# RWKV-7 and HGRN2 layer on one core: the turns of beta,k, of v and of RWKV's outputs made of 32x32 blocks by way of DRAM, and a thread for each pair's end

## The chip, the cores and the metric

One core of a Trainium2 chip. The metric is the device time in microseconds of one launch; the median of three runs counts. Everything is float32; the large products split each operand into a high part (fp32r) and the rest.

## The reference

One layer over T = 512 frames of width 2048 (batch 1):

```
proj = x @ w_in                                      # 512 x 8320
RWKV-7 (16 heads of 64, in the kernel 8 pairs of heads of 128 channels):
  r,k,v,z (+ low-rank decay w and gate a), token shift on all
  S_t = S_{t-1} diag(w_t) + (S_{t-1} a_t) b_t^T + v_t k_t^T ;  o_t = S_t r_t
  o  = groupnorm(o) * gn_w + gn_b + sum(r*k*r_k) * v
  out_r = o * silu(z)
HGRN2 (8 heads of 128): gated linear recurrence, chunkwise; out_h = rmsnorm(o) * g_norm_w * silu(z)
y = [out_r ; out_h] @ w_out
x <- LayerNorm(ALPHA * x + y)
```

## The kernel before

**Stages.** Channels lie on partitions and time on the free axis (128 x 512 tiles). The projections come in units of 128 columns (`proj`, 16 steps of three matmuls each), in the order of `_order()`: for each group of two pairs k, r, v, the z of the group before, then q, f and g of two HGRN heads. Every weight tile (`wr`, 128 x 1024) is loaded on SP's queue and split on chip, half by half, into `wh` (ACT) and `wl` (DVE); there are three buffers of each. A split is asked for one to two parts ahead of its use (`ready`), and the second split of a tile issues the load of the tile after next. After the projections come four output products of 512 columns (`rows`): each has 16 steps, one for each 128 rows of the gated outputs, with 12 matmuls (4 blocks of time, 3 products each).

**RWKV.** `rwkv_prep` makes a pair's operands: `ar` (alpha, r), `bk` (beta, k), both 128 x (8 chunks, 128), the scores `sc`, and turns beta,k and v from channels by time to time by channels, chunk by chunk: `bk` in place, v into rows 64 to 127 of `zz`. `turned` does this without PE: DVE transposes 32 x 32 blocks within each group of partitions (`dtr`), then DMAs between SBUF tiles carry the blocks to their partitions: 16 DMAs of 32 KB for beta,k, 8 for v, in four lots. `rwkv_invert` inverts the triangular part, `from_v` makes the first products of `zz`; `rwkv_scan` goes through the eight chunks of two pairs at once; `outputs` adds what the scores and `zz` give. `rwkv_finish` is a pair's end: mean and variance per head in layout time by channels (`o_all`, in the buffer `ot`), then four identity transposes on PE into a PSUM bank (`tr`, L328), which two scalar_tensor_tensors read together with the weight, `bv`, the bias and the gate; `put_gated` hands the result `g` over. Twelve of the sixteen gated tiles are stored to DRAM (`spill`) and reloaded; RWKV's pairs 6 and 7 and HGRN's heads 6 and 7 stay in `g` buffers, of which there are four.

**Order of work.** All instructions are issued by one planner (class `Plan`) while the program is built. It keeps a clock for each engine, with a cost for each operation, and for each tile the time at which it is ready. The stream of large matmuls is the main line; after each matmul `pump` lets the waiting threads (generators in queues: splits, evacuations, scans, groups, ends, preparations, heads, stores) issue what is due. A PE operation is issued when its operands are due 0.35 us before now, an operation of another engine when they are due within 0.5 us from now. The engines then execute in that order. A thread may wait for room in a pool (`room`), for a tile (`landed`, `by_now`) or for a time. `plan.ready[name] = (time, "dma")` is what the planner takes as landing; on the chip, semaphores hold the readers back until the data is there. All `dma_start` calls of the stretches that matter go through SP's queue, in the order of issue; the planner's `turned` does not look at what else is on that queue.

**The first output product.** At step j, `ahead(j, 0)` splits the gated tile of step j+1 (`split_gated(j + 2)`), whose order is 0 to 5, 8 to 13, 14, 6, 15, 7 (`korder`; 6 and 7 are RWKV's last pairs, 8 and up are HGRN's heads). At step 8 it loads the LayerNorm weights, `lnw` (tile `big`, from `ln_wb`, broadcast to all partitions); from step 11 on it also loads the residual rows (`g<-x_r`). The weight part of step j+2 is split when step j is half issued.

```python
        if d == 0:
            split_gated(j + 2)
            if j == 8:
                plan.until(room(big=1))
                lnw.append(take("big", [P, 2, D]))
                nc.sync.dma_start(lnw[0], ln_wb[None].to_broadcast([P, 2, D]))
```

Of the kernel before, what the change touches and what calls it, by code (L numbers as in the profile page):

```python
# [241 lines left out]
def mixer_kernel(ctx, tc, head, x_r, w_all, par, up, ln_wb, consts, hmask, out):  # L242
# [41 lines left out]
    def drop(*tiles):  # L284
        for t in tiles:
            name = t.tensor.name
            plan.slots[tags.pop(name)].append((plan.used.get(name, plan.count), plan.busy[name][0]))
# [77 lines left out]
    def dtr(o, i):  # L365
        return dve_op([i], o, lambda: dve.transpose(o, i), per=0.0019)
# [22 lines left out]
            f = lambda: dve.tensor_copy(o, i)  # L389
        return Op([act_way(o, i, AF.Copy, scale), ("dve", 0.075 + size(o) * 0.00105 + moved(o, i), f)], [i], [o])  # L390

    def turned(dst, src, tmp, rows=4, base=0):


        name = dst.tensor.name
        yield dtr(tmp, src)
        yield lambda: by_now(tmp)
        for a in range(4):
            for b in range(rows):
                o = base + 32 * b  # L400
                nc.sync.dma_start(dst[o : o + 32, :, 32 * a : 32 * a + 32],
                                  tmp[32 * a : 32 * a + 32, :, 32 * b : 32 * b + 32])
            at = plan.clock["pe"] + 0.4 * rows
            yield lambda: plan.clock["pe"] >= at
        plan.ready[name] = (plan.clock["pe"] + 3.0, "dma")

# [211 lines left out]
            ups.append(upw)  # L620

    hc = [slice(64 * h, 64 * h + 64) for h in range(2)]

    def rwkv_prep(S, p):
        if p == 0:
# [94 lines left out]

        yield room(q4=1)
        tmp = take("q4", [P, NCH, P])
        yield from turned(bk, bk, tmp)
        drop(tmp)
        yield has(S, "v")
        yield room(ksq=2)
        rh, rl = (take("ksq", [P, T], F32R) for _ in range(2))
# [9 lines left out]
        S["bv"] = r  # L737

        yield room(zz=1)
        z = take("zz", [P, NCH, P])  # L740
        yield room(ksq=1)
        tmp = take("ksq")
        yield from turned(z, chunks(v), chunks(tmp), rows=2, base=64)
        drop(v, tmp)
        S["zz"] = z

    def from_v(SS, sc):

        yield lambda: all("zz" in S for S in SS)
        zs = [S["zz"] for S in SS]  # L750
        yield room(main=2, mix=1)
        yield landed(*zs, sc)
        pss = [take("main") for _ in SS]
        for half, (z, ps) in enumerate(zip(zs, pss)):
            for c in range(NCH):
                for h in range(2):
                    yield mm(ps[hc[h], c * C : c * C + C], sc[64:128, 0, half * 16 + 2 * c + h],
                             z[64:128, c, hc[h]])

        def keep():  # L760
            for z, ps in zip(zs, pss):
                for h in range(2):
                    yield copy(z[0:64, :, hc[h]], chunks(ps[hc[h]]))
                drop(ps)

        return keep

    def outputs(SS, sc):

        yield room(mix=2)  # L770
        pss = [take("mix") for _ in SS]
        for half, (S, po) in enumerate(zip(SS, pss)):
            z = S["zz"]
            yield lambda z=z: by_now(z)
            for c in range(0, NCH, 2):
                for h in range(2):
                    for e in range(2):
                        yield mm(po[hc[e], c // 2 * P + 64 * h : c // 2 * P + 64 * h + 64],
                                 sc[:, 1, half * 16 + 2 * (c + e) + h], z[:, c + e, hc[h]])
        for S, po in zip(SS, pss):  # L780
            yield tt(S["o"], S["o"], tiles(po), ALU.add)
            drop(po, S["zz"])
# [49 lines left out]
    def rwkv_scan(SS, sc):  # L832

        pcs, ars, bks, zzs, os = ([S[n] for S in SS] for n in ("pc", "ar", "bk", "zz", "o"))
        yield room(bd=4, rt=2)
        bdss = [[take("bd", [P, P]) for _ in range(2)] for _ in SS]
        rts = [take("rt", [P, P]) for _ in SS]  # L840

        def block(ps, h):
            return ps[hc[h], h * 64 : h * 64 + 64]

        for rt, bds, o in zip(rts, bdss, os):
            yield memset(rt[64:128], 0.0)
            for t in bds:
                yield memset(t, 0.0)
            yield memset(o[0:64, 0], 0.0)
        olds = [None] * 2  # L850
        for c in range(NCH):
            more = c < NCH - 1
            zs = [zz[:, c] for zz in zzs]
            news = [bds[c % 2] for bds in bdss]
            pxs = []
            if c > 0:
                yield landed(*olds)
                yield room(mix=2)
                for ar, old in zip(ars, olds):
                    pxs.append(take("mix"))  # L860
                    yield mm(pxs[-1][:, :P], ar[:, c], old)
                for rt, px, z in zip(rts, pxs, zs):
                    yield stt(rt[0:64], px[0:64, :P], -1.0, z[0:64], ALU.mult, ALU.subtract)
                if more:
                    for new, old, pc in zip(news, olds, pcs):
                        yield act(new, old, AF.Copy, scale=pc[:, c : c + 1])
            else:
                for rt, z in zip(rts, zs):
                    yield copy(rt[0:64], z[0:64], scale=-1.0)
            yield landed(*rts)  # L870
            yield room(mix=2)
            psas = [take("mix") for _ in SS]
            for half, (psa, rt) in enumerate(zip(psas, rts)):
                i = half * 16 + 2 * c
                yield mm(psa[:, :P], sc[:, 0, i : i + 2].rearrange("p h t -> p (h t)"), rt)
            for psa, z in zip(psas, zs):
                for h in range(2):
                    yield copy(z[0:64, hc[h]], block(psa, h))
                drop(psa)
            for px, o in zip(pxs, os):  # L880
                yield copy(o[64 * (c % 2) : 64 * (c % 2) + 64, c // 2], px[64:128, :P])
                drop(px)
            if more:
                yield landed(*zzs)
                yield room(mix=2)
                pds = [take("mix") for _ in SS]
                for pd, bk, z in zip(pds, bks, zs):
                    yield mm(pd[:, :P], bk[:, c], z)
                for pd, new, pc in zip(pds, news, pcs):
                    for h in range(2):  # L890
                        yield stt(new[hc[h], hc[h]], block(pd, h), pc[hc[h], c : c + 1],
                                  new[hc[h], hc[h]], ALU.mult, ALU.add)
                    drop(pd)
                olds = news
        drop(*ars, *bks, *pcs, *rts, *bdss[0], *bdss[1])

    def rwkv_finish(S, p):

        o_all = S["o"]
        yield room(sm=1, ksq=1)  # L900
        og = o_all.rearrange("p j (h i) -> p (j h) i", i=64)
        sm = take("sm", [P, 3, 8])
        sq = take("ksq", [P, 8, 64])
        yield red(sm[:, 0], og)
        yield ts(sm[:, 0], sm[:, 0], 1.0 / 64, None, ALU.mult)
        yield tt(og, og, sm[:, 0, :, None].to_broadcast([P, 8, 64]), ALU.subtract)
        yield act(sq, og, AF.Square)
        yield red(sm[:, 1], sq)
        yield ts(sm[:, 1], sm[:, 1], 1.0 / 64, GN_EPS, ALU.mult, ALU.add)
        yield rsqrt(sm[:, 2], sm[:, 1])  # L910
        yield tt(og, og, sm[:, 2, :, None].to_broadcast([P, 8, 64]))
        drop(sm, sq)
        yield has(S, "z", "bv")
        yield room(g=1, ksq=1)
        g = take("g")
        sz = take("ksq")
        z = S["z"]
        yield landed(o_all)
        po = take("mix")
        for j in range(4):  # L920
            yield tr(po[:, j * P : j * P + P], o_all[:, j])
        yield act(sz, z, AF.Tanh, scale=0.5)
        yield stt(g, po, hcol(HGW, p), S["bv"], ALU.mult, ALU.add)
        drop(po)
        yield stt(z, sz, 1.0, z, ALU.add, ALU.mult)
        yield stt(g, g, hcol(HGB, p), z, ALU.add, ALU.mult)
        drop(z, S["bv"], S["ot"], sz)
        put_gated(p, g)

    def rwkv_group(SS, grp):  # L930
        yield lambda: all("scored" in S for S in SS)
        sc = scores[grp]
        yield from rwkv_invert(SS, sc)

        def run():
            yield from rwkv_scan(SS, sc)
            yield from outputs(SS, sc)
            drop(sc)
            for i, S in enumerate(SS):
                plan.add(finishes, rwkv_finish(S, 2 * grp + i))  # L940

        plan.add(scans[0], run())

# [186 lines left out]


    scans = [plan.queue(), plan.queue()]
    groups, finishes, preps = plan.queue(), plan.queue(), plan.queue()
    heads, stores = plan.queue(), plan.queue()


# [530 lines left out]
```

## Time and profile before

| | |
|---|---|
| median of 3 runs | 1050.75 us (1050.46 to 1051.28) |
| profiled execution | 1050.24 us, of it 1048.5 us from first to last instruction |
| granted TensorE clock | 0.999 |
| PE busy | 1040.6 us (99%), 7342 matmuls |
| DVE, ACT, POOL busy | 755.7 (72%), 437.6 (42%), 38.3 (4%) us |
| DMA moved | 114.79 MB, 56368 of 87305 packets under 512 B |

The profile names a group of instructions by line, engine, operation and tiles (out<-in, buffer numbers left out; a PE matmul names the moving operand, then the stationary one), with count, busy time and the mean duration of one. A line is often that of a helper (L453 the large products in `three`, L324 `mm`, L328 `tr`, L337/L338 ACT passes, L347 tensor_tensor, L356 scalar_tensor_tensor, L366 the block transpose, L401 the DMAs in `turned`, L430 the weight loads), so the tile's name tells the place. The timeline's rows have start, duration, engine, line, what it is, how many were merged, and in brackets how long the engine had been idle and who released it. PE's durations are modelled and overlap; distances between starts are what counts.

### The profile page before, as it was taken

What the parts mean: (1) busy time and instruction counts of PE and PEld (TensorE: products, weight loads), DVE (VectorE), ACT (ScalarE), POOL (GpSimd) and SP (SyncE); (2) the same over time, 40 slices, a digit from 0 to 9 for tenths busy, and PEclk for the clock granted to TensorE, in tenths of its full rate; (3) what the DMA queues carried; (4) which work ended last, traced back from release to release, by engine and by line L of the source; (5) the groups of instructions that cost most, each with busy time, mean ns of one, the idle gap of its engine ahead of it and who ended that gap; (6) DMA issues with size and microseconds to landing.
All of it is one profiled execution on the core that took longest, in us unless ns stands there. A gap on an engine that the chain in (4) does not pass through costs nothing.

```text
span 1048.5 us, 18840 instructions
## 1 busy us (share of the span) xinstructions
PE 1040.6 (99%) x7342; PEld 865.1 (83%) x7342; DVE 755.7 (72%) x1653; ACT 437.6 (42%) x867; POOL 38.3 (4%) x81
## 2 busy tenths in 40 slices
PE   9999999999999999999999999999999999999997
PEld 8888888888888888888888888888888888888885
DVE  7465898667759987676689866865998778625556
ACT  6545333445353354452533353525334554323321
POOL 0000000000000000000000000000000002000000
PEclk9999999999999999999999999999999999999999
DMA  8134342222343522223534323234352244545613
GB/s 332 54 103 114 99 109 86 86 79 81 84 123 100 122 82 74 78 98 79 138 78 118 98 62 96 70 96 110 100 128 72 69 164 131 182 131 159 202 60 131
DMA packets 87305, 114.79 MB, mean 109 GB/s; under 512 B 56368, under 2 KB 58160, under 8 KB 87088
## 3 DMA queue, kind: packets, MB, share of 16 engines
q1 hardware_dynamic: 87072, 113.39, 36.6%
q8 instruction: 58, 0.95, 0.4%
q14 instruction: 31, 0.25, 0.1%
q10 hardware_dynamic: 144, 0.20, 0.1%
HBM read 99.92 MB, written 7.34 MB: 102 GB/s over the span
## 4 chain that ended last, share of the span: by engine, by line
PE 99%; DVE 1%; DVEq 0%; issue 0%
PE main L453 74%; PE mix L324 11%; PE mix L453 8%; PE main L1192 3%; PE main L324 2%; PE mix L328 1%; PE mix L1142 0%; DVE inv L356 0%; DVE inv L347 0%; DVE stats L1549 0%; DVEq L1663 0%; DVE mv L1357 0%; DVE bd L356 0%; DVE mv L352 0%; DVE inv L1140 0%
## 5 line engine op out<-in xcount | busy, mean ns | idle before, releaser
L453 PE MATMUL main<-xl,wh 128*128 128x512 f32 x864 | 341.1, 395 | 0.0
L453 PE MATMUL main<-xh,wl 128*128 128x512 f32 x864 | 341.1, 395 | 0.0
L453 PE MATMUL main<-xh,wh 128*128 128x512 f32 x864 | 340.9, 395 | 0.0
L337 ACT ACTIVATE wh<-wr 128x512 fp32r<-128x512 f32 x299 | 186.9, 627 | 237.1 <-PE main L453 180.5
L347 DVE TENSOR_TENSOR wl<-wr,wh 128x512 fp32r<-128x512 f32 x299 | 203.8, 682 | 61.8 <-ACT wh L337 60.1
L453 PEld LDWEIGHTS main<-xh,wh 128*128 128x128 f32 x864 | 162.4, 188 | 33.0
L453 PEld LDWEIGHTS main<-xh,wl 128*128 128x128 f32 x864 | 162.5, 188 | 32.6
L453 PEld LDWEIGHTS main<-xl,wh 128*128 128x128 f32 x864 | 162.4, 188 | 32.6
L453 PE MATMUL main<-wl,xh 128*128 128x512 f32 (+1 forms) x262 | 102.6, 392 | 0.0
L453 PE MATMUL main<-wh,xh 128*128 128x512 f32 (+1 forms) x262 | 102.1, 390 | 0.0
L453 PE MATMUL main<-wh,xl 128*128 128x512 f32 (+1 forms) x262 | 101.6, 388 | 0.0
L453 PEld LDWEIGHTS main<-wh,xh 128*128 128x128 f32 x262 | 49.2, 188 | 9.9
L453 PEld LDWEIGHTS main<-wh,xl 128*128 128x128 f32 x262 | 49.2, 188 | 9.7
L453 PEld LDWEIGHTS main<-wl,xh 128*128 128x128 f32 x262 | 49.2, 188 | 9.6
L338 ACT ACTIVATE t<-main,om 128x512 f32<-128x512 f32 x33 | 22.4, 687 | 51.1 <-PE main L453 41.6
L356 DVE SCALAR_TENSOR_TENSOR t<-main,pr,t 128x511 f32<-128x511 f32 x33 | 24.4, 747 | 26.5 <-ACT t L338 26.2
L347 DVE TENSOR_TENSOR inv<-inv,inv 64x30 f32<-64x30 f32 (+14 forms) x120 | 38.6, 322 | 2.9
L347 DVE TENSOR_TENSOR inv<-inv 64x30 f32<-64x30 f32 (+14 forms) x120 | 38.4, 320 | 2.3
L347 DVE TENSOR_TENSOR t<-t,tot 128x256 f32<-128x256 f32 x96 | 37.8, 414 | 1.8 <-PE mix L324 1.7
L356 DVE SCALAR_TENSOR_TENSOR bd<-mix,pc,bd 64x64 f32<-64x64 f32 x112 | 31.7, 283 | 7.5 <-PE mix L324 5.2
L337 ACT ACTIVATE zz<-mix 64x64 f32<-64x64 f32 x63 | 13.8, 220 | 46.9 <-PE mix L324 45.8
L338 ACT ACTIVATE t<-main 128x512 f32<-128x512 f32 x32 | 18.5, 598 | 30.7 <-PE main L453 30.2
(222 smaller groups left out, 1328.0 us busy)
## 6 DMA issues: line engine op xcount, KB each, us to landing
wr<-w_all SPq DMA_DIRECT2D x156, 512.0 KB, 3.6
q<-head SPq DMA_DIRECT2D x15, 448.0 KB, 5.9
q<-q SPq DMA_DIRECT2D x128, 32.0 KB, 2.4
g<-x_r SPq DMA_DIRECT2D x16, 256.0 KB, 3.8
spill<-g SPq DMA_DIRECT2D x12, 256.0 KB, 2.7
out<-q SPq DMA_DIRECT2D x12, 256.0 KB, 2.4
t<-spill SPq DMA_DIRECT2D x10, 256.0 KB, 4.2
zz<-ksq SPq DMA_DIRECT2D x64, 32.0 KB, 2.6
```

Source lines behind the costliest of these rows:

```text
L324: return Op([("pe", cost, lambda: pe.matmul(o, l, r, start=start, stop=stop, **kw))], [l, r], [o], mode="narrow" if narrow else "main" if ...
L328: return Op([("pe", 0.11, lambda: pe.transpose(o, i, ident))], [i], [o])
L337: return "act", cost, lambda: sc_e.activation(o, i, f, scale=scale)
L338: return "act", cost, lambda: sc_e.activation(o, i, f, scale=scale, bias=bias)
L347: return dve_op([a, b], o, lambda: dve.tensor_tensor(o, a, b, f), base=0.16 if o.shape[0] < P and size(o) == C and o.tensor.name in tags e ...
L356: return dve_op([a, b], o, lambda: dve.scalar_tensor_tensor(o, a, s, b, f1, f2), per=0.00113, base=0.085 if o.shape[0] == P else 0.25 if s ...
L453: pe.matmul(ps, l, r, start=first and i == 0, stop=last and i == 2)
L1192: pe.matmul(pss[a], *ops, start=k == 0 and low == of == 0, stop=k == KT - 1 and low == 1)
```

## The change

`turned` now makes a turn of a tile of c chunks by n groups of 32 columns in three steps: one `dtr` whose output lies block column by block column; one DMA of the whole tile to a new DRAM tile `far`; then, 4.4 us of planned PE time later, n DMAs back (4 for beta,k and for an end, 2 for v), each bringing one block row to 32 partitions, with contiguous pieces of c x 32 numbers. The planner takes the target as ready 4.7 us after these are issued. The turned layout has block columns outside and chunks inside: (a, c, f) in place of (c, a, f). `zz` is kept in that layout and its readers use strided views; beta,k is copied by ACT or DVE into the other layout, into the buffer that held the block transpose. In `rwkv_finish` the four PE transposes go: `o_all` is block-transposed into `g`, goes by way of DRAM back into `ot`, one ACT pass applies weight and bias while reordering, and two tensor_tensors add `bv` and multiply by the gate. The queue of ends becomes two queues, one for each pair of a group.

```diff
+    def turned(dst, src, tmp, base=0):
+        c = src.shape[1]
+        n = src.shape[2] // 32
+        yield dtr(tmp, src.rearrange("p c (b f) -> p b c f", f=32))
         yield lambda: by_now(tmp)
-        for a in range(4):
-            for b in range(rows):
-                o = base + 32 * b
-                nc.sync.dma_start(dst[o : o + 32, :, 32 * a : 32 * a + 32],
-                                  tmp[32 * a : 32 * a + 32, :, 32 * b : 32 * b + 32])
-            at = plan.clock["pe"] + 0.4 * rows
-            yield lambda: plan.clock["pe"] >= at
-        plan.ready[name] = (plan.clock["pe"] + 3.0, "dma")
+        far = dpool.tile([4, 32, n, c * 32], F32, tag=nm("far"), name=nm("far"))
+        nc.sync.dma_start(far.rearrange("a p b r -> (a p) b r"), tmp.rearrange("p b c f -> p b (c f)"))
+        plan.busy[tmp.tensor.name] = (plan.clock["pe"] + 4.4, "dma")
+        at = plan.clock["pe"] + 4.4
+        yield lambda: plan.clock["pe"] >= at
+        for b in range(n):
+            o = base + 32 * b
+            nc.sync.dma_start(dst[o : o + 32].rearrange("p a c f -> p a (c f)"),
+                              far[:, :, b].rearrange("a p r -> p a r"))
+        plan.ready[dst.tensor.name] = plan.busy[dst.tensor.name] = (plan.clock["pe"] + 4.7, "dma")
...
-        yield from turned(bk, bk, tmp)
-        drop(tmp)
+        flat = bk.rearrange("p c t -> p (c t)")
+        yield from turned(blocks(flat, NCH), bk, blocks(tmp.rearrange("p c t -> p (c t)"), NCH))
+        yield copy(tmp.rearrange("p c (a f) -> p a c f", f=32), blocks(flat, NCH))
+        drop(bk)
+        S["bk"] = tmp
...
-        z = take("zz", [P, NCH, P])
+        z = take("zz", [P, 4, NCH, 32])
...
-        yield from turned(z, chunks(v), chunks(tmp), rows=2, base=64)
+        yield from turned(z, chunks(v), blocks(tmp, NCH), base=64)
...
-                             z[64:128, c, hc[h]])
+                             z[64:128, hb[h], c])
...
-        yield room(g=1, ksq=1)
+        yield room(g=1)
         g = take("g")
+        yield from turned(blocks(S["ot"], 4), o_all, blocks(g, 4))
+        yield room(ksq=1)
         sz = take("ksq")
         z = S["z"]
-        yield landed(o_all)
-        po = take("mix")
-        for j in range(4):
-            yield tr(po[:, j * P : j * P + P], o_all[:, j])
         yield act(sz, z, AF.Tanh, scale=0.5)
-        yield stt(g, po, hcol(HGW, p), S["bv"], ALU.mult, ALU.add)
-        drop(po)
+        yield act(in_blocks(g), blocks(S["ot"], 4).rearrange("p a c f -> p c a f"), AF.Identity,
+                  scale=hcol(HGW, p), bias=hcol(HGB, p))
         yield stt(z, sz, 1.0, z, ALU.add, ALU.mult)
-        yield stt(g, g, hcol(HGB, p), z, ALU.add, ALU.mult)
+        yield tt(g, g, S["bv"], ALU.add)
+        yield tt(g, g, z)
...
-                plan.add(finishes, rwkv_finish(S, 2 * grp + i))
+                plan.add(finishes[i], rwkv_finish(S, 2 * grp + i))
...
-    groups, finishes, preps = plan.queue(), plan.queue(), plan.queue()
+    groups, finishes, preps = plan.queue(), [plan.queue(), plan.queue()], plan.queue()
```

The other readers and writers of `zz` (`from_v`, `outputs`, `rwkv_scan`) change their views in the same way.

More of the change, by code (lines that the diff above doesn't have):

```diff
@@ L390, in copy, with in_blocks, blocks @@
         return Op([act_way(o, i, AF.Copy, scale), ("dve", 0.075 + size(o) * 0.00105 + moved(o, i), f)], [i], [o])
-    def turned(dst, src, tmp, rows=4, base=0):
-        name = dst.tensor.name
-        yield dtr(tmp, src)
+    def turned(dst, src, tmp, base=0):
+        c = src.shape[1]
+        n = src.shape[2] // 32
+        yield dtr(tmp, src.rearrange("p c (b f) -> p b c f", f=32))
         yield lambda: by_now(tmp)
-        for a in range(4):
-            for b in range(rows):
-                o = base + 32 * b
-                nc.sync.dma_start(dst[o : o + 32, :, 32 * a : 32 * a + 32],
-                                  tmp[32 * a : 32 * a + 32, :, 32 * b : 32 * b + 32])
-            at = plan.clock["pe"] + 0.4 * rows
-            yield lambda: plan.clock["pe"] >= at
-        plan.ready[name] = (plan.clock["pe"] + 3.0, "dma")
+        far = dpool.tile([4, 32, n, c * 32], F32, tag=nm("far"), name=nm("far"))
[8 more added lines that the diff above has]
+        plan.ready[dst.tensor.name] = plan.busy[dst.tensor.name] = (plan.clock["pe"] + 4.7, "dma")
+    def in_blocks(t):
+        return t.rearrange("p (c a f) -> p c a f", a=4, f=32)
+    def blocks(t, c):
+        return t.rearrange("p (a c f) -> p a c f", c=c, f=32)
     splits = plan.queue()
@@ L622, in mixer_kernel @@
     hc = [slice(64 * h, 64 * h + 64) for h in range(2)]
+    hb = [slice(2 * h, 2 * h + 2) for h in range(2)]
     def rwkv_prep(S, p):
@@ L762, in keep @@
                 for h in range(2):
-                    yield copy(z[0:64, :, hc[h]], chunks(ps[hc[h]]))
+                    yield copy(z[0:64, hb[h]], ps[hc[h]].rearrange("p (c a f) -> p a c f", c=NCH, f=32))
                 drop(ps)
@@ L778, in outputs @@
                         yield mm(po[hc[e], c // 2 * P + 64 * h : c // 2 * P + 64 * h + 64],
-                                 sc[:, 1, half * 16 + 2 * (c + e) + h], z[:, c + e, hc[h]])
+                                 sc[:, 1, half * 16 + 2 * (c + e) + h], z[:, hb[h], c + e])
         for S, po in zip(SS, pss):
@@ L843, in block, with by32 @@
             return ps[hc[h], h * 64 : h * 64 + 64]
+        def by32(t):
+            return t.rearrange("p (a f) -> p a f", f=32)
         for rt, bds, o in zip(rts, bdss, os):
@@ L852, in rwkv_scan @@
             more = c < NCH - 1
-            zs = [zz[:, c] for zz in zzs]
+            zs = [zz[:, :, c] for zz in zzs]
             news = [bds[c % 2] for bds in bdss]
@@ L862, in rwkv_scan @@
                 for rt, px, z in zip(rts, pxs, zs):
-                    yield stt(rt[0:64], px[0:64, :P], -1.0, z[0:64], ALU.mult, ALU.subtract)
+                    yield stt(by32(rt[0:64]), by32(px[0:64, :P]), -1.0, z[0:64], ALU.mult, ALU.subtract)
                 if more:
@@ L868, in rwkv_scan @@
                 for rt, z in zip(rts, zs):
-                    yield copy(rt[0:64], z[0:64], scale=-1.0)
+                    yield copy(by32(rt[0:64]), z[0:64], scale=-1.0)
             yield landed(*rts)
@@ L877, in rwkv_scan @@
                 for h in range(2):
-                    yield copy(z[0:64, hc[h]], block(psa, h))
+                    yield copy(z[0:64, hb[h]], by32(block(psa, h)))
                 drop(psa)
```

## The prediction

> **What bounds the kernel now.** I read the page first: busy times, then the chain that ended last, then who waited for whom on PE. From the page:
>
> ```profile
> PE 1040.6 (99%) x7342; PEld 865.1 (83%) x7342; DVE 755.7 (72%) x1653; ACT 437.6 (42%) x867; POOL 38.3 (4%) x81
> PE 99%; DVE 1%; DVEq 0%; issue 0%
> ```
>
> All waits of PE, and two pieces of the chain:
>
> ```profile
> PE mix L324 <- ACT ksq L1409: 1.5, 1, 1.5
> PE mix L1142 <- DVE inv L1140: 1.1, 1, 1.1
> PE mix L324 <- DVE bd L356: 0.4, 1, 0.4
> ...
> 893.81 13.43 PE main L453 x59
> 907.23 43.52 PE mix L453 x192
> ```
>
> PE is never out of work: its three waits come to 3.0 us, 1.1 at the start and 1.5 in the closing normalisation. So there are two ways to change the time: give PE less to do, or make it wait. DVE (72%) and ACT (42%) set the time only where PE stands and waits for them. One large matmul costs PE 43.52/192 = 0.2267 us; I use this, not the modelled durations, which overlap.
>
> **What the change takes from PE.** The four identity transposes of each pair's end go (`tr` in rwkv_finish). On PE's timeline such a batch reads:
>
> ```profile
> 280.48 0.39 PE L453 MATMUL main<-xh,wl 128*128 128x512 f32 x1
> 280.71 0.60 PE L328 MATMUL mix<-cst,t 128*128 128x128 f32 x4
> 281.06 0.48 PE L453 MATMUL main<-xh,wh 128*128 128x512 f32 x1
> 281.38 0.40 PE L453 MATMUL main<-xl,wh 128*128 128x512 f32 x1
> ...
> 893.21 0.60 PE L328 MATMUL mix<-cst,t 128*128 128x128 f32 x4
> ```
>
> Three starts later, 0.90 us have gone where two large matmuls need 0.45, so a batch costs 0.45 us, its change of kind included. I looked at all eight (first and last shown): each stands alone between large matmuls, so none keeps its change of kind when it goes. Sum: 8 x 0.45 = **-3.6 us**.
>
> **What it changes in PE's other work.** The matmuls that read `zz` now read runs of 32 columns 1 KB apart. No row shows that pattern; the nearest are short strided runs and plain ones:
>
> ```profile
> L324 PE MATMUL mix<-zz,q 128*128 128x128 f32 x112 | 17.2, 276 | 0.0
> L324 PE MATMUL mix<-zz,big 128*64 128x64 f32 x256 | 8.3, 224 | 0.0
> L324 PE MATMUL main<-zz,big 64*64 64x64 f32 x256 | 8.3, 220 | 0.0
> L324 PE MATMUL mix<-t 128*32 128x16 f32 x512 | 5.9, 185 | 0.0
> L324 PE MATMUL mix<-q,t 128*32 128x48 f32 x256 | 3.6, 208 | 0.0
> ```
>
> Plain reads lie on a line: (276-208)/80 = 0.85 ns a column, hence 181 ns for 16. The strided 16 take 185, 4 ns more. Over 112+256+256 = 624 matmuls that is +2.5 us at most; nothing at least, since a longer run can't be worse than a short one. I take 0: 4 ns is noise, and the runs here are longer.
>
> **DVE, ACT and the queues.** The block transposes of beta,k and v stay; one of 128x512 per end is new:
>
> ```profile
> L366 DVE STREAM_TRANSPOSE q<-q x8: 1231/1234/1239, 72.7 to 755.9; 128x1024 f32<-128x1024 f32 x8
> L366 DVE STREAM_TRANSPOSE ksq<-t x8: 698/700/706, 83.4 to 771.4; 128x512 f32<-128x512 f32 x8
> ```
>
> DVE gets 8 x 0.70 for it; two scalar_tensor_tensors per end become two tensor_tensors of the same size (0). ACT gets one 128x512 pass per end, 8 x 0.63 (row at 890.50 below). The new 128x1024 copy of beta,k is about two such passes on either engine, 8 x 1.3. Some 16 us in all on two engines with 255 and 611 us free: no time, as long as nobody waits in line behind them. POOL gets nothing. SP issues 5 + 3 + 5 = 13 DMAs per pair for 16 + 8 = 24, larger ones. What transfers take over the run, issue to landing:
>
> ```profile
> wr<-w_all SPq DMA_DIRECT2D x156, 512.0 KB, 3.6
> q<-q SPq DMA_DIRECT2D x128, 32.0 KB, 2.4
> spill<-g SPq DMA_DIRECT2D x12, 256.0 KB, 2.7
> t<-spill SPq DMA_DIRECT2D x10, 256.0 KB, 4.2
> zz<-ksq SPq DMA_DIRECT2D x64, 32.0 KB, 2.6
> big<-ln_wb SPq DMA_DIRECT2D x1, 2048.0 KB, 10.1
> ```
>
> A store lands in 2.7 to 3.6 and the code leaves 4.4 us for it; the returns (256 KB, or 512 KB in four pieces) come in about 4, where it leaves 4.7. So landings hold in ordinary stretches, and beta,k and v are done up to 4 us later than now. For v the margin is these rows of `zz`:
>
> ```profile
> L401 SPq DMA_DIRECT2D zz<-ksq x64: 585/608/1270, 86.8 to 778.3; - x64
> L337 ACT ACTIVATE zz<-main x8: 591/592/594, 182.1 to 800.6; 64x512 f32<-64x512 f32 x8
> ```
>
> The last block is issued at 778.3, and the first product read from it is evacuated at 800.6: some 18 us to spare. I put 0 there. What is new in kind: before, only PE read a turned tile. Now ACT or DVE copies beta,k and ACT scales the end straight from the landing, and both run in order: if it is late, all behind them is.
>
> **The one stretch where a landing is late.** It is the ends of pairs 6 and 7, beside the first output projection. That has 16 steps of 12 matmuls (2.72 us); its last ends at 907.23, so step 12 starts at 896.35 and step 13 at 899.07. Step 13 needs pair 6's gated output, step 15 pair 7's. DVE's timeline (sum of pair 6, its normalisation's last step, its gated output, that of pair 7), then SP's and ACT's:
>
> ```profile
> 872.67 0.68 DVE L360 TENSOR_REDUCE sm<-t 128x8 f32<-128x512 f32 x1
> ...
> 878.83 0.69 DVE L347 TENSOR_TENSOR t<-t,sm 128x512 f32<-128x512 f32 x1
> ...
> 883.33 0.75 DVE L356 SCALAR_TENSOR_TENSOR g<-g,half,t 128x512 f32<-128x512 f32 x1
> ...
> 895.28 0.75 DVE L356 SCALAR_TENSOR_TENSOR g<-g,half,t 128x512 f32<-128x512 f32 x1
> ```
>
> ```profile
> 884.70 0.33 SPq L430 DMA_DIRECT2D wr<-w_all  x1
> 885.13 1.26 SPq L1473 DMA_DIRECT2D big<-ln_wb  x1
> 890.09 0.33 SPq L430 DMA_DIRECT2D wr<-w_all  x1
> ```
>
> ```profile
> 890.50 0.63 ACT L337 ACTIVATE wh<-wr 128x512 fp32r<-128x512 f32 x1 [1.60 <-PE main L453]
> 891.04 0.62 ACT L337 ACTIVATE xh<-g 128x512 fp32r<-128x512 f32 x1
> 893.18 0.63 ACT L337 ACTIVATE wh<-wr 128x512 fp32r<-128x512 f32 x1 [1.00 <-PE main L453]
> 893.72 0.61 ACT L337 ACTIVATE xh<-g 128x512 fp32r<-128x512 f32 x1
> 896.54 0.63 ACT L337 ACTIVATE wh<-wr 128x512 fp32r<-128x512 f32 x1 [2.21 <-DMA wr<-w_all]
> ```
>
> Of the weight loads that SP issues between 880 and 900:
>
> ```profile
> DMA to landing us min/median/max: 3.7/4.2/6.3
> ```
>
> The 2 MB of `ln_wb` go out at 885.13 and land at 895.2. The load issued at 890.09 is the 6.3: it lands at 896.4 behind them, and ACT waits 2.2 us for it. What is issued after `ln_wb` arrives after it.
>
> Now pair 6 after the change. Its normalisation ends at 879.5 as before, or up to a microsecond later, as pair 7 now shares DVE. Transpose to 880.2; the store goes out at about 880.8 and lands by 883.6. The returns follow 4.4 us after it, 885.2 at the earliest, and `ln_wb` belongs to the start of step 8, issued some 0.4 us earlier than now, since pair 6's batch on PE is gone: 884.7. So the returns queue behind 2 MB and land not at 889.9, as the order of work assumes, but between 895.2 and about 897; I take 896.4, like the weight load.
>
> PE reaches steps 12 and 13 by then 0.9 us sooner relative to this (two batches gone): 895.45 and 898.2. Lower end: pair 6 alone is late. Scale, two DVE passes, split, 0.6 each: 896.4 + 2.4 = 898.8, a wait of **0.6**. Upper end: the scale stands in ACT's order ahead of the weight split of 890.50 and the split of 891.04, both wanted by step 12. It does, if the planner lets it go half a microsecond ahead of 889.9, as it may; that weight split belongs to the middle of step 10, 891.4 by then. ACT then stands still until 896.4, and works off scale, weight split, gated split by 898.2; DVE does pair 6's two passes and two subtractions by 899.5, of which step 12's third matmul, 0.45 in, needs the last: step 12 starts at 899.1, a wait of **3.7**. (Pair 7's returns, about 3 us later, block ACT again, but PE is late by then itself.) The row of 890.50 against 889.9 puts me near the upper end: **+3.5**.
>
> **Sum:** -3.6 + 3.5 = -0.1. The profiled execution took 1050.24 (span 1048.5 and 1.7 around it), 0.5 under the median 1050.75 of the three runs; it becomes about 1050.1, and against the median 1050.7. A difference under 0.2% (2.1 us) is about what this kernel's measurement can't tell from none.
>
> **Rivals.** First, *full gain*: the returns are there in time, because they slip ahead of `ln_wb` (half a microsecond decides) or because it clears the rings sooner. With the 4.2 us of an ordinary 256 KB load they would land at 889.4, nobody waits, and the time is 1050.75 - 3.6 = 1047.1. Against it stands the 10.1 us row and the load of 6.3 behind it. The Trainium skill, *DMA: Bandwidth & Descriptors*, section "Anatomy of one DMA", gives a transfer as about 2.0 us plus bytes over 436 GB/s (a fit for GpSimd's path); my estimate from it is 6.8 us for `ln_wb`, which would end at 891.9, the returns near 893, and the stall would all but vanish. This trace's 10.1 us disagrees, and decides. Chance of this rival 0.28, partial gains beyond 2.1 us included.
>
> Second, *SP held*: pair 7's store falls behind `ln_wb` too, lands at about 896.4, and its returns stand in SP's order ahead of the weight load of 890.09. SP then waits at the returns, and that load goes out at 896.4 + 4 x 0.33 = 897.7 for 890.09, landing 3.7 later at 901.4 against 896.4. Split by 902.7, it feeds step 14, due at 895.45 + 5.44 = 900.9, or 904.6 with the stall above. By itself +1.8; where ACT is held by pair 7's scale (returns landing near 901) ahead of that split, step 13's split waits for it too, 902.5 + 0.7 for a step due at 898.2: +5.0 in place of 3.5, and with the +1 us of a returns' landing at 897.4 about +6: time 1050.75 - 3.6 + 6 = 1053.2. It decides once pair 7's returns precede that load; pair 7's normalisation is 2 to 4 us behind pair 6's, so its returns belong near 889 to 891, just about there. Chance 0.16.
>
> Third, *the copies starve the scan*: beta,k land late at several of the eight pairs, a blocked DVE makes PE's next scan matmul wait. For it: one wait for `bd` (0.4) exists already. Against: sizes and times above. 0.3 us at each of 16 landings, +4.8: 1051.9. With strided reads at their +2.5 added, 1054. Chance 0.04 for slower.
>
> **Chances.** Within 0.2%: 0.52, my forecast of a gain given back (0.6 to 3.7 us of wait and the small unknowns). Faster 0.28; slower 0.20 (second and third). The range takes in the full gain and the second rival: 1047.0 to 1053.3; the forecast's own is 1048.6 to 1051.9.
>
> **What would show it.** Right: L328 x56 in place of x88; 13 DMAs a pair; PE's waits grow by 2 to 4 us, all between 890 and 905, on `wh`, `xh` or `wl`, and behind them ACT waiting for the returns of the end. Wrong: no wait there (full gain), or waits in the scan on `rt`, `bd` or `zz` (third rival), or a weight load that stands at SP for a store (second).

## The result, and the profile after

The changed kernel takes **1066.97 us** (median of 4 runs, 1064.92 to 1070.04); the kernel before took 1050.61 (4 runs on the same chip). The ratio is 1.0158, 95% interval 1.0131 to 1.0184. The predicted 1050.7 and its range to 1053.3 were wrong: the change costs 16 us.

The profiled execution is the slowest of the four: 1070.04 us, of it a span of 1067.2, which is 18.7 more than the span before (1048.5). The page of the changed kernel, busy times and the chain that ended last:

```profile
PE 1047.3 (98%) x7310; PEld 866.9 (81%) x7310; DVE 760.4 (71%) x1660; ACT 449.6 (42%) x884; POOL 39.0 (4%) x81
PE 83%; DMA 6%; DVE 6%; ACT 2%; issue 1%; SPq 1%; POOL 0%; DVEq 0%; ACTq 0%
```

Before, PE made up 99% of the chain. Now 6% of it are transfers and 6% DVE: again and again the work that ended last runs through a landing. PE's waits in the changed kernel (total us, times, longest):

```profile
PE main L464 <- ACT xh L337: 3.3, 1, 3.3
PE mix L324 <- ACT ksq L337: 2.8, 2, 1.9
PE mix L324 <- issue: 2.2, 2, 1.5
PE mix L324 <- ACT ksq L1426: 1.5, 1, 1.5
PE mix L324 <- DVE ksq L347: 1.3, 3, 0.5
PE main L464 <- ACT wh L337: 1.3, 1, 1.3
PE mix L1159 <- DVE inv L1157: 1.1, 1, 1.1
PE mix L324 <- ACT zz L337: 0.7, 1, 0.7
PE main L464 <- DVE wl L347: 0.3, 1, 0.3
```

They come to 14.5 us in place of 3.0 (+11.5). Only the 1.5 at L1426 and the 1.1 are the old ones. That is not all: behind four of the waits the granted clock is at half for 3.4 us each. Stretches of the changed kernel, with busy time (and count) of PE, PEld, DVE, ACT and POOL, then granted clock, DMA share and GB/s:

```profile
186.60:190.00 3.40, 3.40 (x9) 2.61 (x8) 2.76 (x10) 2.13 (x6) 0.00 (x0) 0.51 0.02 5
562.10:565.50 3.40, 3.40 (x10) 2.65 (x9) 3.09 (x8) 0.00 (x0) 0.00 (x0) 0.50 0.00 0
777.10:780.50 3.40, 3.40 (x9) 2.65 (x8) 3.30 (x9) 0.28 (x1) 0.00 (x0) 0.51 0.30 119
913.70:917.10 3.40, 3.27 (x8) 2.57 (x9) 3.10 (x5) 1.64 (x4) 0.00 (x0) 0.50 0.90 222
```

In 3.4 us PE does 8 to 10 matmuls here, where 15 fit at 0.2267 us each. About half of 4 x 3.4 us is lost: 6.8. PE looks fully busy in these stretches, so busy time doesn't show the loss; the column of the clock does.

**Where it begins: beta,k.** A landing of beta,k in the changed kernel, first on SP, then on ACT, then on PE (start, duration, engine, line, what; in brackets the idle time before and its releaser):

```profile
320.94 0.33 SPq L441 DMA_DIRECT2D wr<-w_all  x1
321.32 0.42 SPq L401 DMA_DIRECT2D far<-q  x1
326.20 0.33 SPq L441 DMA_DIRECT2D wr<-w_all  x1
326.63 1.79 SPq L407 DMA_DIRECT2D q<-far  x4
```

```profile
332.78 1.06 ACT L337 ACTIVATE q<-q 128x1024 f32<-128x1024 f32 x1 [5.68 <-DMA q<-far]
333.74 0.61 ACT L337 ACTIVATE wh<-wr 128x512 fp32r<-128x512 f32 x1
334.26 0.61 ACT L337 ACTIVATE ksq<-t 128x512 fp32r<-128x512 f32 x1
```

```profile
334.93 0.49 PE L324 MATMUL mix<-ksq,ones_r 128*128 128x512 f32 x1 [0.92 <-ACT ksq L337]
335.97 0.50 PE L324 MATMUL mix<-ksq,ones_r 128*128 128x512 f32 x1 [0.55 <-DVE ksq L347]
```

The store stands behind a 512 KB weight load issued 0.4 us before it, and lands 5.1 us after its issue, at 326.4, where 4.4 are booked. Six of the eight stores of beta,k go out like that, and land after 5.0 to 5.3 us; the other two, 1.2 and 4.7 us behind a load, after 3.7 and 3.8. SP has to wait for the landing before it may issue the returns, and issues them from 326.63 to 328.0 and not from 325.7. But the store isn't what decides here: the weight load of 326.20 stands ahead of the returns in SP's order, and had itself waited 4.7 us for a DVE instruction (for its buffer, which a split sets free), so an earlier landing of the store would not have brought the returns forward. `e13` below shows that. The last return lands at 332.67, 6.0 after the first one's issue; 4.7 are booked. By the booking the tile is there at 321.3 + 4.4 + 4.7 = 330.4; it comes 2.3 us later. The copy stands next in ACT's order, so ACT stands still for 5.7 us; the weight split and the `ksq` split behind it are late, and PE, which has nothing to do with beta,k here, waits 1.5 us for `ksq`, in two pieces. The same happens at 558.4 (waits of 1.85 and 0.23, then half clock at 562.1) and at 773.3 and 775.6 (1.79, half clock at 777.1).

**The last ends.** The chain that ended last, changed kernel (start, duration, what):

```profile
897.38 9.39 DMA far<-g
...
908.53 2.08 DMA t<-far
...
910.79 0.82 ACT g L338
...
913.15 0.64 ACT xh L337
```

SP's rows beside it:

```profile
896.90 0.38 SPq L1490 DMA_DIRECT2D big<-ln_wb  x1
897.38 0.38 SPq L401 DMA_DIRECT2D far<-g  x1
900.60 0.33 SPq L441 DMA_DIRECT2D wr<-w_all  x1
906.86 2.11 SPq L407 DMA_DIRECT2D t<-far  x4
```

Pair 6's store goes out half a microsecond behind the 2 MB of `ln_wb` and lands after 9.4 us. SP stands at it until 906.8, and the split of the gated output, `xh`, ends at 913.8: PE waits 3.35 us and runs at half clock from 913.7 on.

**The sum against the span's +18.7:** three landings of beta,k, 5.3 us of waits and two half-clock stretches, 3.4; the last end 3.35 + 1.7; waits of PE for nothing that the profile shows ("issue"), 2.2 + 1.7; the two small waits (0.7, 0.3) less one of before (0.4), +0.6; the transposes left out, -3.5. Together +14.7. **Some 4 us I could not assign**; about half of it lies in stretches of small matmuls.

### The profile page after: what moved, and what is told of

Read it like the earlier page. It is cut to its first block, busy times and chain, and to the rows that moved or that the text cites. A ratio compares the mean times of both kernels' runs of the same rounds, so it can differ in the third digit from the quotient of the medians.

```text
span 1067.2 us, 18725 instructions
## 1 busy us (share of the span) xinstructions
PE 1047.3 (98%) x7310; PEld 866.9 (81%) x7310; DVE 760.4 (71%) x1660; ACT 449.6 (42%) x884; POOL 39.0 (4%) x81
## 4 chain that ended last, share of the span: by engine, by line
PE 83%; DMA 6%; DVE 6%; ACT 2%; issue 1%; SPq 1%; POOL 0%; DVEq 0%; ACTq 0%
PE main L464 60%; PE mix L324 10%; PE mix L464 8%; PE main L1209 3%; DMA wr<-w_all 3%; PE main L324 2%; DMA q<-far 1%; DVE wl L347 1%; DMA far<-g 1%; DVE inv L366 1%; SPq L407 1%; DMA t<-far 1%; DVE t L347 1%; DMA far<-q 0%; PE mix L328 0%
## 5 line engine op out<-in xcount | busy, mean ns | idle before, releaser
L356 DVE SCALAR_TENSOR_TENSOR t<-main,pr,t 128x511 f32<-128x511 f32 x33 | 24.4, 746 | 18.0 <-ACT t L338 17.7
L338 ACT ACTIVATE t<-main 128x512 f32<-128x512 f32 x32 | 18.7, 597 | 42.7 <-PE main L464 42.6
```

What stands on the lines that cost most here:

```text
L338: return "act", cost, lambda: sc_e.activation(o, i, f, scale=scale, bias=bias)
L356: return dve_op([a, b], o, lambda: dve.scalar_tensor_tensor(o, a, s, b, f1, f2), per=0.00113, base=0.085 if o.shape[0] == P else 0.25 if s ...
```

## The experiments

The theory: landings later than booked hold up ACT, which works in order; PE waits behind it, and behind some of the waits its clock is halved. Rivals: the copies, one part of the change alone, `ln_wb` alone, the changed order of work itself. Each kernel was timed beside the kernel before on the same chip; ratios are to that.

**The two parts alone.** `e1_ends_only` has `turned` as before for beta,k and v and sends only the ends through DRAM, with the two queues; `e2_turns_only` has the turns through DRAM and the ends as before.

```diff
 e1: -        yield from turned(blocks(flat, NCH), bk, ...); yield copy(...)
     +        yield from turned(bk, bk, tmp)          # between SBUF tiles, as before
 e2: -        yield from turned(blocks(S["ot"], 4), o_all, blocks(g, 4))
     +            yield tr(po[:, j * P : j * P + P], o_all[:, j])   # as before
```

> Only the ends of the pairs are turned by way of DRAM (and have a thread each); beta,k and v are turned between SBUF tiles as before, with their old layouts and no copy. Theory A (an ACT or DVE instruction that reads straight from a late landing holds its engine, and PE then starves): the waits around beta,k's copies (at 334, 449, 558 and 773 us of the changed kernel) are gone, the one beside the first output product (910 us) stays: 3 to 5 us of PE waits and a halved clock behind them, less 3.6 us of transposes, 1050 to 1054 us. Theory B (PE pays for another order of work: instruction supply in longer runs of small matmuls and more changes of kind, whatever lands when): waits of 1 to 2 us 'on nothing' stay, 1052 to 1056, spread over the kernel.

> Only beta,k and v are turned by way of DRAM; the ends keep their four PE transposes and their one thread. Theory A: the waits at beta,k's copies stay, the one at 910 us goes, L328 x88: slower than before by 8 to 14 us, 1058 to 1064. If all the loss sat in the ends, beside the load of the LayerNorm weights, it would be within 2 us of before.

Measured: e1 1067.68 us (1.0165, 1.0150 to 1.0180), e2 1063.15 us (1.0111, 1.0096 to 1.0126). Each part alone loses about as much as both: 17.1 and 12.5 against 16.4. The losses don't add, so this isn't a price for each operation; it is one of being late somewhere. e2 came out as expected; e1 is 12 us above the higher of its expectations, since ends in the middle of the kernel were late too (PE waits 2.5 and 1.0 us at 295 to 299), where the changed kernel has no wait. In e1, ACT waits 31.4 us for returns of the ends; in e2, 24.4 us for those of beta,k. In e1 one store's landing at 286.96 was followed by the issue of its returns only at 292.25, as SP was busy with the 32 KB DMAs of a turn, most of them 0.61 us each where the planner books 0.4.

**Without the copy.** `e3_no_copy` lets beta,k come back in 16 smaller returns straight in the old layout:

```diff
-        yield from turned(blocks(flat, NCH), bk, ...); yield copy(...)
+        yield from turned(bk, bk, blocks(...), inner=True)   # 16 returns of 32 KB
```

> As changed, but beta,k come back from DRAM straight into their old layout (16 returns of 32 KB in pieces of 128 bytes), so that no ACT or DVE pass reads from the landing; PE alone does. Theory A: the waits at 334, 449, 558 and 773 us go, 1054 to 1059 us, though the landings are no earlier. Theory B, or if it is the traffic: 1064 to 1070 as changed.

Measured: 1062.33 us (1.0112, 1.0097 to 1.0127). 4.6 us less than the changed kernel, but 11.7 above before, and between the two expectations. The copy, the third rival's culprit, is at most a part: ACT now waits 26.7 us at the scaling of the ends instead.

**Later bookings and `ln_wb`, each alone and together.**

```diff
 e4: -  4.4 (store), 4.7 (return)      +  5.9, 7.2
 e5: -            if j == 8:           +            if j == 14:     # ln_wb's load
 e6: both
```

> As changed, but the planner waits 5.9 us for the store and counts on the return 7.2 us after its issue (4.4 and 4.7 before), so copies and scales stand later in their engines' order. Theory A: waits at beta,k's copies shrink to under 1 us each, the one at 910 us stays, 1054 to 1060 us. Theory B: 1064 to 1070 us.

> As changed, but the 2 MB of LayerNorm weights are loaded at step 14 of the first output product instead of step 8, behind the returns of the last two ends. Theory A (late landings that ACT or DVE stand at): the wait at 910 us and the halved clock behind it go, all others stay: about 6 us less than changed, 1059 to 1063 us. If that wait had another cause than the queue, it stays: 1065 to 1070.

> Both: planned 5.9 and 7.2 us, and the LayerNorm weights at step 14. Theory A: no wait is left but the two that the kernel before has, and the eight batches of transposes are gone: 1046.5 to 1048.5 us, faster than before. If the new order itself costs (more changes of kind, instruction supply): 1049 to 1052.

Measured: e4 1054.58 us (1.0033, 1.0019 to 1.0047); e5 1063.69 (1.0114, 1.0084 to 1.0143); **e6 1048.43 (11 runs; 0.9976, 0.9968 to 0.9985)**, faster than both, and than the kernel before. Later bookings are worth 12.4 us. `ln_wb` is worth 6.2 with them and 3.3 without; the 3.3 is rough, as e5's runs (1056.8 to 1066.3) overlap those of the changed kernel. What is left in e4 is the one place at `ln_wb`, its PE row and the stretch behind it:

```profile
898.94 0.80 PE L464 MATMUL main<-wh,xh 128*128 128x512 f32 x1 [3.37 <-ACT xh L337]
```

```profile
897.80:904.60 6.80, 5.66 (x13) 4.42 (x14) 4.85 (x8) 3.47 (x6) 0.00 (x0) 0.50 0.72 214
```

The clock fell to half at 897.8, still within the wait, so that PE's 13 matmuls from 898.94 on lost 2.7 us by it. Wait and clock come to 6.1; less the 0.7 that e6 still waits at this place, that is 5.4, as much as the spans of the two profiled executions differ (1052.0 and 1046.6). PE's waits in e6:

```profile
PE mix L324 <- ACT ksq L1426: 1.5, 1, 1.5
PE mix L1159 <- DVE inv L1157: 1.1, 1, 1.1
PE main L464 <- ACT xh L337: 0.7, 1, 0.7
PE mix L324 <- issue: 0.2, 1, 0.2
```

ACT's waits for returns fell from 36.3 us (23.2 + 9.7 + 3.4) to 4.4, and no stretch at half clock is left before the last 2 us. The transfers didn't get much faster (stores of beta,k still land after 2.6 to 5.5 us, their returns after 2.5 to 6.5); their readers now stand later in the order.

**Is the gain of e6 only `ln_wb`'s place?** `e12_before_ln_moved` is the kernel before with `if j == 14`.

> The kernel before with nothing changed but the LayerNorm weights at step 14: a control. PE does not wait there before, so 1050.2 to 1051.2 us by every theory; if it is faster, part of the gain of the moved load has nothing to do with the turns.

Measured: 1050.55 us (1.0000, 0.9991 to 1.0009). By itself the move does nothing.

**The parts alone with later bookings.** `e7_ends_later_ln_moved` is e1, and `e14_turns_later` is e2, each with bookings of 5.9 and 7.2 and with `j == 14`.

> The ends alone by way of DRAM (beta,k and v between SBUF tiles as before), planned 5.9 and 7.2 us, LayerNorm weights at step 14. Theory A: the gain is all in the ends, so as fast as with all three turned, 1046.5 to 1048.5, unless the 192 transfers of 128-byte pieces make the ends' landings later than 7.2 us now and then, 1049 to 1054.

> Only beta, k and v go by way of DRAM, with landings booked at 5.9 and 7.2 us; the scan's ends keep their PE transposes, in one queue; ln_wb's load moved. With before at 1050.6, the same with ln_wb moved at 1050.55, the ends alone at 1052.7 and both parts at 1048.4, this is the fourth corner. Theory A (the gain of the version with both parts is that of the 32 PE transposes left out, 3.5 us of PE's small work, and the turns bring nothing by themselves): 1050 to 1052. Rival (the turns carry the gain, by freeing SP's queue from the strided copies): 1048 to 1049.5.

Measured: e7 1052.72 us (1.0021, 1.0012 to 1.0030), e14 1053.14 us (1.0024, 1.0015 to 1.0034). Both are slower than before by a little, while both parts together are faster: neither expectation for e14 was met, and e7 met the second of its own, though not by late landings (ACT waits 3.1 us for the returns there). PE's waits in e14:

```profile
PE mix L324 <- DVE bd L356: 1.6, 1, 1.6
PE mix L324 <- ACT ksq L1427: 1.5, 1, 1.5
PE mix L324 <- issue: 1.1, 2, 0.7
PE mix L1160 <- DVE inv L1158: 1.1, 1, 1.1
```

The 1.6 stands in a scan, with a half-clock stretch behind it in this execution; 1.1 of "issue" is new. e7 has all of the transposes' gain and four new waits of 0.4 to 1.2 us (3.8 together, by the trace). Every edit makes the planner write another order, and a new wait or two weigh as much as the 3.5 us that the edit saves.

**One queue of ends.** `e8_one_thread` is e6 with a single queue for the ends.

> As with both margins and the moved load, but one queue for the ends of both pairs as in the kernel before. Theory A: pair 7's end then starts when pair 6's is done, some 20 us after it; its gated output is due 6.7 us after it was ready before, so PE waits 5 to 15 us at step 14 or 15 of the first output product: 1053 to 1064. If ends have slack: 1046.5 to 1048.5.

Measured: 1106.81 us (1.0536, 1.0520 to 1.0552), far above what I expected. PE waits 22.6 us for `xh` and 13.6 for `t`, and half-clock stretches come to 58 us. In the trace the large matmuls stop from 833 to 868. My reading, from the planner's code: the ends follow one another with 13 us of planned landings each, hold their buffers, and two evacuations of PSUM wait for a `t` buffer. With these bookings, the second thread is what makes the long round trip bearable.

**One booking later.** `e9_return_later` is e5 with only 4.7 to 7.2, `e10_store_later` e5 with only 4.4 to 5.9.

> LayerNorm weights at step 14; the store planned with 4.4 us as changed, the return with 7.2 instead of 4.7. Between 1063.7 us (4.4 and 4.7) and 1048.4 (5.9 and 7.2): if it is the instruction that stands at the return that counts (theory A), this takes the larger part, 1048.5 to 1053 us; if it is SP that stands at the store and holds weight loads and returns back, 1056 to 1064.

> LayerNorm weights at step 14; the store planned with 5.9 us instead of 4.4, the return with 4.7 as changed. Theory A: the landing of the return, 4.3 to 4.7 us after the last of four issues that take 1.4 us, is still later than 4.7: 1053 to 1062 us. If it is SP at the store: 1048 to 1052.

Measured: e9 1071.01 us (1.0194, 1.0178 to 1.0209), e10 1065.77 (1.0144, 1.0130 to 1.0158). Both are slower than either of their expectations, and they don't tell which booking matters: the planner put the last scan's end 87 and 50 large matmuls later than in e5, so that the last ends miss the first output product (PE waits 13.7 and 8.6 us for `xh` there). A change of one booking also changed the order.

**The order of the last steps.** `e11_order` is e6 with the gated tiles 14, 15, 6, 7 last, in place of 14, 6, 15, 7.

> As with both margins and the moved load (1048.4 us), but the first output product takes the gated tiles in the order ... 14, 15, 6, 7 instead of ... 14, 6, 15, 7, which gives pair 6's end one more step of 2.7 us. The one wait left beside those of the kernel before, 0.7 us on pair 6's split, goes: 1047 to 1048.2 us. If the last wait is not pair 6's landing, no change.

Measured: 1048.3 us (0.9980, 0.9971 to 0.9989). The wait of 0.7 for `xh` shrank to 0.2, and the time stayed as in e6.

**The order kept, the data less.** e9 and e10 had left open whether late landings or the new order itself cost the time. `e13_less_moved` is e5, instruction for instruction in the same order, but a store and its returns carry only the first 32 columns of each block column: an eighth of beta,k, a quarter of the ends, v whole. The rest of the turned beta,k and ends is left out.

```diff
-        nc.sync.dma_start(far..., tmp...)
+        part = 32 if base == 0 else c * 32
+        nc.sync.dma_start(far...[:, :, :part], tmp...[:, :, :part])   # the returns likewise
```

> The changed kernel with ln_wb's load moved (the order of e5, whose median was 1063.7 us and whose profiled execution took 1056.8), every instruction in the same order on every engine, but of each block of 256 columns of beta and k, and of 128 columns of the scan's ends, only the first 32 columns travel to DRAM and back (v travels whole). So most of the turned beta, k and ends are left out; the transfers are fewer bytes, the order is untouched. Theory A (landings later than booked, in an order that holds): the waits of ACT on the far landings (25.1 and 5.0 us in e5) fall below 8 us, PE's waits go back to 3 to 5 us, no stretch at half clock, and the time falls to 1048 to 1051. Rival (the order itself is worse, by more small matmuls together): the time stays at 1057 to 1066 with the same stretches of small matmuls.

Measured: 1052.38 us (1.0017, 1.0008 to 1.0027; single runs 1049.89 to 1053.84), 11.3 less than e5 with the same order, and between the two expectations. PE's waits:

```profile
PE mix L324 <- issue: 1.9, 2, 1.5
PE mix L324 <- ACT ksq L1426: 1.5, 1, 1.5
PE mix L1159 <- DVE inv L1157: 1.1, 1, 1.1
PE mix L324 <- ACT zz L337: 0.7, 1, 0.7
PE main L464 <- ACT wh L337: 0.6, 1, 0.6
PE main L464 <- DVE wl L347: 0.5, 2, 0.3
```

The waits for `ksq` that beta,k caused are gone. That shows the larger part: 11.3 of the 13.1 us that e5 lost come with the data that beta,k and the ends move, not with the order. And e6 moves all of that data and loses nothing, so it isn't the traffic by itself either: it is early bookings and long landings together. The size is rough: e5's runs spread over 9.5 us, its profiled execution was the fastest of them, and no trace shows the waits of the others. About 4 us over e6 remain in an order with early bookings, of which the trace shows 1.9 of "issue" and one half-clock stretch behind it (186.4, 1.7 us). ACT's waits for beta,k fell only from 25.1 us to 13.0, where I had expected under 8: a small return also waits behind a 512 KB load in its queue (it lands after 3.4 to 3.6 us when issued 0.4 behind one, after 2.5 when 1.4 behind). And at the three landings that made PE wait the returns go out no sooner: 5.3 to 5.4 us after the store, as in the changed kernel, though the store now lands after 3.7. There SP comes to them behind the weight load; what the smaller data brought forward is the last return's landing, 2.6 to 2.9 us after its issue and not 4.7 to 5.8.

## Why the prediction was wrong

**The transposes: right.** L328 goes from x88 to x56. Taken over the trace (from the large matmul ahead of each group of small ones to the second behind it, less 0.45), the work that isn't large matmuls is 147.3 us before and 143.9 in e6: -3.4, where -3.6 was forecast.

**Strided reads of `zz`: right.** The groups in the changed kernel:

```profile
L324 PE MATMUL mix<-zz,q 128*128 128x128 f32 x112 | 17.4, 275 | 0.7 <-ACT zz L337 0.7
L324 PE MATMUL mix<-zz,big 128*64 128x64 f32 x256 | 8.3, 224 | 0.0
L324 PE MATMUL main<-zz,big 64*64 64x64 f32 x256 | 8.3, 220 | 0.0
```

275, 224 and 220 ns are the 276, 224 and 220 of before. The 0 for v's landing held too: the wait of 0.7 for `zz` stands behind two table loads of 1.28 us in ACT's order, not behind a landing.

**Busy times of DVE and ACT: no matter, but miscounted.** The terms written out (5.6, 5.0 and 10.4) come to 21 us, not 16, and DVE had 293 us free, not 255. Measured are +4.7 on DVE and +12.0 on ACT.

**"So landings hold in ordinary stretches": the step that failed.** By it the landings of beta,k were no term of the sum. I set the medians of other transfers (2.7 to 3.6, "about 4") against the bookings. The medians of the changed kernel are themselves beyond that, and that of beta,k's stores beyond the booking of 4.4:

```profile
far<-q SPq DMA_DIRECT2D x8, 512.0 KB, 5.0
q<-far SPq DMA_DIRECT2D x32, 128.0 KB, 4.5
far<-ksq SPq DMA_DIRECT2D x8, 256.0 KB, 4.4
```

Three things were left out. A store of 512 KB goes behind a weight load of 512 KB in the same queue, and so do the returns at half of the landings; I had reckoned with queueing only at `ln_wb`. Four returns take SP 1.8 us to issue, so the last lands 6 us and more after the first one's issue, and the booking counts from the first. And the returns stand in SP's order behind a weight load that waits for its buffer. At the three landings that made PE wait, the last return lands 11.3 to 12.5 us after the store's issue; 9.1 were booked, and 13.1 in e4 and e6. I wrote down that ACT works in order and that "all behind them is" late, and then priced this, as the third rival, at 0.3 us a landing with a chance of 0.04. Measured: 5.3 us of PE's waits, at three of eight landings of beta,k, plus the clock. They were not at `rt`, `bd` or `zz` in the scan, where that rival looked, but at `ksq` and `wh`, the splits behind the copy.

**The halved clock was no term at all.** Every wait in the sum counted once. Four of them here brought 1.7 us more, the one in e4 2.7: the wait of about 3.5 that I forecast at the last ends cost 5.0 in the changed kernel and 6.1 in e4.

**The last ends: place and size of the wait right, the chain not.** Forecast +3.5 for the returns behind `ln_wb`; measured 3.35, but for the store behind it. I had the store 3.9 us ahead of that load (880.8 and 884.7); it went out 0.5 behind it. The step that is off is pair 6's normalisation, which I let end at "879.5 as before, or up to a microsecond later". Its last step in the changed kernel:

```profile
895.00 0.69 DVE L347 TENSOR_TENSOR t<-t,sm 128x512 f32<-128x512 f32 x1
```

It ends 1.2 us ahead of `ln_wb`'s issue at 896.90; before, it ended 5.6 ahead (879.5 and 885.13). So SP stood at the store, as in the second rival, which had it for pair 7, though the weight load of 900.60 was out by then. `ln_wb` took 9.2 us, against the 6.8 estimated from the Trainium skill, *DMA: Bandwidth & Descriptors*, section "Anatomy of one DMA", whose fit is for GpSimd's path; this load goes by SP's.

**Waits for nothing that the profile shows** (2.2 us of "issue") I had not thought of. The wait at 183.9 stands in a run of small matmuls, 128 of 128x16, 64 of 64x64 and 64 of 32x32; e6 has the 128 some 8 us earlier and doesn't wait there. A 16 KB packet of the queue named "instruction" starts just behind 183.0 and takes 0.95 us, so late instructions are a guess; no run shows the cause.

**The full gain** needed landings that hold. With them, e6 gains 2.5 us (1.6 to 3.4, by its ratio) and not 3.6: waits of 0.7 and 0.2 are new, 0.4 went, which makes 3.0 of the 3.5; the rest is within the interval.

## What to carry to other kernels

A time that a planner books for a transfer has to hold what stands ahead of it, in the queue and in the issuing engine's order, and the issue of all its pieces, not the median of a transfer by itself: here 5.9 + 7.2 us in place of 4.4 + 4.7 took 12 of the 16 us away, and with the 2 MB load moved as well, +16 became -2. Before a landing's reader is put on an engine that works in order, look at what stands behind it there: a copy that nobody needs yet stopped the splits that PE needed at once. And PE paid for some short waits twice, so read the clock's column beside the waits.

## What the runs showed of the hardware

**Half clock behind short waits, though not behind all.** In stretches full of large matmuls, each wait of PE of 2.0 us or more in these runs had a stretch at a granted clock of 0.5 behind it or from within it on; the stretches last 3.4 us, or 6.8, 10.2, 13.7 and 34.1. Of the waits between 1.0 and 1.9 us some had one (1.01 in e1 at 614.7, in a run of small matmuls; 1.5 and 1.85 in the changed kernel; 1.55 in e14) and some had none (1.85 in e1 at 514.1, 1.86 in e5, 1.1, 1.1 and 1.2 in e7; nor had the 0.9 and 0.55 close together at 334 in the changed kernel). The Trainium skill, *TensorE: Matmul & The Clock Gate*, section "Why this matters for your kernels", advises against idle gaps over some 3 us; in these runs half clocks stand behind shorter ones too. Its section "What's actually happening" has a free-running window of 3.4 us, which would fit the lengths seen; what decides between two waits of 1.85 us no run here shows.

**The spread of e5 goes with the clock.** The four runs of e5 took 1056.8, 1063.0, 1064.4 and 1066.3 us at mean granted clocks of 0.997, 0.995, 0.994 and 0.992. By the clock alone, the 0.005 between the first and the last is 5.3 of their 9.5 us. The kernel before spreads over 1 us, e6 over 1.7.
